# Seven-product output projection: weight sums made earlier and kept in DRAM, y combinations made beside the attention output, evictions in steps

## The chip, the cores and the metric

One core of one Trainium2 chip runs the whole program. The time is device microseconds (us) of one execution; runs are compared by their median. The engines are named as in the profile: PE is TensorE (matmuls; PEld are its weight loads), DVE is VectorE, ACT is ScalarE, POOL is GpSimd, and SP is SyncE, whose queue issues all the transfers of this kernel.

## The reference

A decoder layer on 512 tokens of width 2048: an attention branch and a gated delta branch run beside each other, are merged by two sigmoid gates, and go through an output projection. What matters here is the end of each:

```python
    y_a = a_out @ w_o_swa
    ...
    y_b = o.reshape(B, T, DN_VAL).astype(x.dtype) @ w_o_dn

    y = jax.nn.sigmoid(mg_a) * y_a + jax.nn.sigmoid(mg_b) * y_b
    return x + gate * (y @ w_out)
```

`w_out` is 2048 x 2048, `w_o_dn` 4096 x 2048, `w_o_swa` 2048 x 2048, all float32.

## The kernel before, in words

**Precision.** Every large product is made of three fp32r matmuls (`mm3`, lines 221 to 226): each operand is split into a high and a low part (`split`, lines 50 to 53: a cast on ACT, a subtraction on DVE), and high x high, high x low and low x high are added in PSUM.

**Weights.** `plan` (line 141) writes out one list of jobs, each a weight tile of 128 x 2048. `load_job` (179) loads a job into one of two buffers `raw`; `split_half` (188) splits half of it (1024 columns) into one of three pairs `whi`, `wlo`; `half` hands a half out by name. Loads and splits are set off by `half_done` and `weight_tick`, so that they run ahead of the matmuls: a load is issued when the second half of the job two before it has been split.

**Order of work.** The program is laid out by hand as a sequence of tiles (`channel_tile`, 228: 16 blocks kt of three matmuls, 48 in all). After every second kt it calls `pump` (81), which gives other work, written as generators, its next step: `go` by a count of ticks, `paced` by a budget per tick against the cost that the generator yields, `beside` by a rate. This sets the order in which the instructions are written down; the compiler's scheduler then puts each engine's queue in an order of its own, and may bring an instruction forward when its buffer and its data are free.

**Stages.** Start, delta branch, then three stages at the end that the change touches:

- *Delta output* (`branch_b`, 924). Twice (`half`): 16 blocks of the delta branch's output are loaded as `oraw` (line 938, two buffers) and split into `oh` and `ol`; two merge gate tiles `ma`; then 16 tiles `od`, whose matmuls need all 16 blocks. The first half's results go to `yb_d` in DRAM, the second half adds to them. Beside it `gate` (1418) loads 16 tiles `gw` of 1 MB, one buffer, and adds each to `gate_bc` on DVE.
- *Attention output* (`finish`, 1213). 16 tiles `os`. Each tile j is merged with its gates into y (128 channels x 512 tokens, `m`) and stored to `y_d`. y is cut in four quadrants (channels below and above block 8, tokens `lo` and `hi`), and of the seven left factors of the product scheme five are made and split here: a11, s3, a12, s1, s2.
- *Output projection* (`output`, 1277). y @ w_out by a scheme with seven products m1 to m7 of half-size matrices instead of eight, for each of two column blocks n. An item is one quarter of a product (p, 2 kt, 12 matmuls); 2 x 7 x 4 items. The right factors are quadrants of `w_out` and four sums of them: the sums are made on DVE in place just ahead of their split (`add`, line 1297; `prep`, 1317), in the buffers a, b and c, loaded by `load` (1290). The last two left factors a22 and s4 are made meanwhile by `combos` (1254) from `y_d`: loads of `ya` and `yc`, sums and low parts on POOL (1272, 1274, 1263), casts on ACT (1262). `evict` (1358) combines a finished product with the ones kept; `columns` (1349) multiplies by the gate (DVE, 1352), loads x (1354), adds it on POOL (1355) and stores (1356). A product's whole eviction is written down at one point, in the middle of the first item after it.

Of the kernel before, what the change touches and what calls it, by code (L numbers as in the profile page):

```python
# [7 lines left out]
F32 = mybir.dt.float32  # L8
# [8 lines left out]
P = 128  # L17
# [15 lines left out]
NFIRST = 4  # L33
STW = 320 + NST * P


class Layer:
# [103 lines left out]
    def plan(self):  # L141
# [28 lines left out]
        jobs += [(f"out{i}", a["w_out"][0, i]) for i in range(2)]  # L170
# [90 lines left out]
    def build(self):  # L261
        tc, nc, a = self.tc, self.nc, self.a
        with ExitStack() as es:
# [4 lines left out]
            self.v_d = self.dram.tile([2, P, T], F32, name="v_d")  # L268
            self.wraw = es.enter_context(tc.tile_pool(name="wraw", bufs=2, reuse_waits="tile"))
# [654 lines left out]
    def branch_b(self):  # L924
        tc, nc, a = self.tc, self.nc, self.a
        with ExitStack() as es:
# [5 lines left out]
            self.beside(self.gate(wk, pg), 0.2, "gate")  # L932
            oh = op.tile([P, KT, T], F32R, name="oh")
# [20 lines left out]
            self.drain("gate")  # L954
        self.dump("yb", self.yb_d)


# [255 lines left out]
    def finish(self):  # L1213
        tc, nc, a = self.tc, self.nc, self.a
        with ExitStack() as es:
# [4 lines left out]
            yp.tile([P, 504], F32, name="aligny")  # L1220
            lo, hi = slice(0, 256), slice(256, 512)
            with ExitStack() as eo:
                self.pmm = eo.enter_context(tc.tile_pool(name="pmmf", bufs=2, space=PSUM, reuse_waits="tile"))
                for j in range(KT):
# [10 lines left out]
                    nc.sync.dma_start(out=self.y_d[j], in_=m)  # L1235
                    put = lambda n, src: self.split(A[n][0][:, j % 8, :], A[n][1][:, j % 8, :], src)
                    put("a11" if j < 8 else "a12", m[:, lo])
                    if j < 8:
                        nc.vector.tensor_tensor(out=yb[:, lo], in0=m[:, lo], in1=m[:, hi], op=ALU.add)
                        put("s3", yb[:, lo])  # L1240
                    else:
# [8 lines left out]
            for n in ("a22", "s4"):  # L1250
                A[n] = quad(fx, n)
            self.output(es, wk, fx, A)

    def combos(self, wk, A):

        nc = self.nc
        lo, hi = slice(0, 256), slice(256, 512)
        TT = nc.gpsimd.tensor_tensor

        def put(n, kt, src):  # L1260
            h, l = A[n][0][:, kt, :], A[n][1][:, kt, :]
            nc.scalar.copy(out=h, in_=src)
            TT(out=l, in0=src, in1=h.bitcast(F32), op=ALU.subtract)

        for kt in range(8):
            p = wk.tile([P, T], F32, tag="m", name="ya")
            nc.sync.dma_start(out=p, in_=self.y_d[kt])
            q = wk.tile([P, T], F32, tag="yb", name="yc")
            nc.sync.dma_start(out=q, in_=self.y_d[kt + 8])
            yield  # L1270
            put("a22", kt, q[:, hi])
            TT(out=p, in0=p, in1=q, op=ALU.subtract)
            yield
            TT(out=p[:, lo], in0=p[:, lo], in1=p[:, hi], op=ALU.add)
            put("s4", kt, p[:, lo])

    def output(self, es, wk, fr, A):
# [3 lines left out]
        slots = {}  # L1281

        def load(slot, c, r, nchunk, parts=(0, 1)):

            for i in parts:
                if slot == "a":
                    t = self.wraw.tile([P, 2048], F32, tag="raw", name="raw")
                else:
                    t = fr.tile([P, 2048], F32, tag=f"{slot}{i}", name=f"raw{slot}")
                nc.sync.dma_start(out=t, in_=a["w_out"][2 * c + nchunk, 2 * r + i])  # L1290
                slots[slot, i] = t

        piece = lambda slot, p: slots[slot, p // 2][:, (p % 2) * 1024 : (p % 2) * 1024 + 1024]

        def add(x, y):
            def f(p):
                nc.vector.tensor_tensor(out=piece(x, p), in0=piece(x, p), in1=piece(y, p), op=ALU.add)

            return f

# [222 lines left out]
```

## Time and profile before

| | |
|---|---|
| median of 3 runs | 2995.43 us (2982.93 to 2997.62) |
| profiled execution | 2993.07 us, its span 2991.3 us |
| PE busy | 2881.6 us, 96% |
| DVE busy | 1790.8 us, 60% |
| ACT busy | 1084.1 us, 36% |
| POOL busy | 281.9 us, 9% |
| moved by DMA | 450.07 MB, mean 150 GB/s |

Times are microseconds from the first instruction. "Busy" is the sum of an engine's instructions; matmuls are pipelined, so that a new one starts every 0.23 us though each lasts 0.39. A groups row has the line, engine and operation, the tiles out<-in, shapes and count, then busy us and mean ns of one, then the idle time of the engine just before them and what ended it. A waits row reads "who line <- what it waited for: us in total, times, longest". The stages lie at about 1683 to 2082 us (delta output), 2640 to 2807 (attention output) and 2807 to the end (output projection).

### The profile page before, as it was taken

The page shows a single profiled execution, that of the slowest core. Times are in us where ns is not written, and L with a number is a line of the kernel's source. Part 1 is how long each engine was busy: PE and PEld are TensorE (multiplying, and loading weights), DVE is VectorE, ACT ScalarE, POOL GpSimd, SP SyncE. Part 2 cuts the span into 40 slices and gives each one's busy share as a digit, 9 for nine tenths or more (in the row PEclk, how much of TensorE's full clock was granted, in tenths as well). Part 3 has the DMA queues.
Part 4 walks back from the last instruction along what each step waited for, and adds up shares of the span by engine and source line. Part 5 has one row for each costly group of instructions (what it writes and reads, how often), then busy time and mean ns, then how long its engine had stood idle before and what let it go on. Part 6 is the DMA issues. An engine that isn't in the chain of part 4 may idle for free.

```text
span 2991.3 us, 37937 instructions
## 1 busy us (share of the span) xinstructions
PE 2881.6 (96%) x14524; PEld 2358.0 (79%) x14524; DVE 1790.8 (60%) x2863; ACT 1084.1 (36%) x2101; POOL 281.9 (9%) x236
## 2 busy tenths in 40 slices
PE   6899989999999999999999999999999999999988
PEld 5587777778788888888888788888788788888767
DVE  5765898898544444455544453433755655554787
ACT  3355333333433333333333322312234434432333
POOL 0012220210000000001000000000100000000251
PEclk8999999999999999999999999999999999999999
DMA  9855635633533333343332575555322223355652
GB/s 335 308 173 176 182 130 168 187 102 121 154 125 107 121 107 124 113 136 113 123 124 85 190 265 197 200 167 164 104 87 87 74 101 101 112 202 183 217 169 85
DMA packets 175079, 450.07 MB, mean 150 GB/s; under 512 B 74129, under 2 KB 76689, under 8 KB 139057
## 3 DMA queue, kind: packets, MB, share of 16 engines
q1 hardware_dynamic: 174898, 447.66, 45.4%
q8 instruction: 114, 1.87, 0.3%
q14 instruction: 67, 0.55, 0.1%
HBM read 385.90 MB, written 59.46 MB: 149 GB/s over the span
## 4 chain that ended last, share of the span: by engine, by line
PE 77%; DVE 10%; DMA 6%; POOL 2%; issue 2%; ACT 2%; SPq 1%; POOLq 0%; DVEq 0%; ACTq 0%
PE mm L224 21%; PE mm L226 21%; PE mm L225 21%; DVE wlo L53 2%; DVE atmp L708 2%; DVE A L714 1%; DMA E<-g_rows 1%; DVE wa L390 1%; PE S L1150 1%; ACT whi L52 1%; PE O L1201 1%; PE pv L861 1%; PE po L880 1%; PE pP L258 1%; DMA oraw<-o_d 1%
## 5 line engine op out<-in xcount | busy, mean ns | idle before, releaser
L224 PE MATMUL mm<-hh,whi 128*128 128x512 f32 x2784 | 1136.6, 408 | 0.7 <-ACT mth L247 0.7
L226 PE MATMUL mm<-hh,wlo 128*128 128x512 f32 x2784 | 1094.2, 393 | 0.0
L225 PE MATMUL mm<-hl,whi 128*128 128x512 f32 x2784 | 1093.1, 393 | 0.0
L53 DVE TENSOR_TENSOR wlo<-raw,whi 128x1024 fp32r<-128x1024 f32 (+1 forms) x452 | 555.4, 1231 | 501.3 <-ACT whi L52 486.4
L52 ACT CAST whi<-raw 128x1024 fp32r<-128x1024 f32 (+1 forms) x452 | 470.6, 1043 | 947.8 <-PE mm L225 894.6
L226 PEld LDWEIGHTS mm<-hh,wlo 128*128 128x128 f32 x2784 | 525.5, 189 | 113.7 <-issue 0.4
L224 PEld LDWEIGHTS mm<-hh,whi 128*128 128x128 f32 x2784 | 527.0, 189 | 110.6 <-issue 8.4
L225 PEld LDWEIGHTS mm<-hl,whi 128*128 128x128 f32 x2784 | 527.8, 190 | 99.7 <-issue 0.8
L224 PE MATMUL mm<-oh,whi 128*128 128x512 f32 x512 | 200.6, 393 | 2.0 <-ACT oh L52 1.0
L225 PE MATMUL mm<-ol,whi 128*128 128x512 f32 x512 | 199.6, 390 | 1.0 <-DVE ol L53 1.0
L226 PE MATMUL mm<-oh,wlo 128*128 128x512 f32 x512 | 199.5, 390 | 0.5 <-DVE wlo L53 0.5
L808 POOL TENSOR_TENSOR qe<-qe,yq 128x512 f32<-128x512 f32 x32 | 50.1, 1586 | 929.0 <-DMA qe<-eg_rows 868.7
L677 POOL TENSOR_TENSOR E<-E,neg_g 128x512 f32<-128x512 f32 x64 | 76.1, 1189 | 488.0 <-DMA E<-g_rows 416.1
L224 PEld LDWEIGHTS mm<-oh,whi 128*128 128x128 f32 x512 | 96.2, 188 | 24.0 <-ACT oh L52 2.0
L225 PEld LDWEIGHTS mm<-ol,whi 128*128 128x128 f32 x512 | 96.2, 188 | 22.6 <-DVE ol L53 2.0
L226 PEld LDWEIGHTS mm<-oh,wlo 128*128 128x128 f32 x512 | 96.2, 188 | 21.0 <-DVE wlo L53 1.2
L708 DVE TENSOR_TENSOR atmp<-A 128x62 f32<-128x62 f32 (+30 forms) x124 | 111.0, 895 | 2.0
L714 DVE TENSOR_TENSOR A<-A,atmp 128x62 f32<-128x62 f32 (+30 forms) x124 | 109.5, 883 | 1.8
L854 DVE SCALAR_TENSOR_TENSOR r<-pp,neg_eg,vt 128x128 f32<-128x128 f32 x96 | 29.2, 346 | 81.2 <-PE pp L851 79.4
L553 DVE SCALAR_TENSOR_TENSOR yv<-mm,convh,yv 128x511 f32<-128x511 f32 (+2 forms) x96 | 71.4, 744 | 8.1 <-ACT yv L550 6.7
L1174 ACT ACTIVATE sm<-sm,mx,rs 128x256 f32<-128x256 f32 (+1 forms) x128 | 71.7, 562 | 3.3 <-DVE mx L1169 3.3
L390 DVE SCALAR_TENSOR_TENSOR wa<-wa,silu_cb 128x2048 f32<-128x2048 f32 x24 | 54.8, 2282 | 7.1 <-DMA silu_cb<-silu_d 7.1
(350 smaller groups left out, 3179.4 us busy)
## 6 DMA issues: line engine op xcount, KB each, us to landing
raw<-in_w_ch SPq DMA_DIRECT2D x158, 1024.0 KB
wa<-in_w_ada_ss SPq DMA_DIRECT2D x32, 1024.0 KB
raw<-in_w_od SPq DMA_DIRECT2D x32, 1024.0 KB
E<-g_rows SPq DMA_DIRECT2D x64, 256.0 KB
gw<-in_w_ada_gate SPq DMA_DIRECT2D x16, 1024.0 KB
raw<-in_w_os SPq DMA_DIRECT2D x16, 1024.0 KB
qe<-eg_rows SPq DMA_DIRECT2D x32, 256.0 KB
o_d<-zh SPq DMA_DIRECT2D x32, 256.0 KB
```

Of the source, the lines that this page charges most:

```text
L52: self.nc.scalar.copy(out=hi, in_=src)
L53: self.nc.vector.tensor_tensor(out=lo, in0=src, in1=hi.bitcast(F32), op=ALU.subtract)
L224: nc.tensor.matmul(ps, lhsT=wh, rhs=xh, start=first, stop=False)
L225: nc.tensor.matmul(ps, lhsT=wh, rhs=xl, start=False, stop=False)
L226: nc.tensor.matmul(ps, lhsT=wl, rhs=xh, start=False, stop=last)
L390: nc.vector.scalar_tensor_tensor(out=wa, in0=wa, scalar=1.0, in1=scb, op0=ALU.mult, op1=ALU.mult, accum_out=t[:, j : j + 1])
L553: nc.vector.scalar_tensor_tensor(out=y[:, s:], in0=ps[:, : T - s], scalar=w[:, j : j + 1], in1=y[:, s:], op0=ALU.mult, op1=ALU.add)
L677: nc.gpsimd.tensor_tensor(out=E, in0=E, in1=ng, op=ALU.add)
L708: eng.tensor_tensor(out=t, in0=A[:, m : m + 1, m + 1 :].to_broadcast([P, m, n]), in1=A[:, :m, m : m + 1].to_broadcast([P, m, n]), op=ALU.mult,
L714: eng.tensor_tensor(out=A[:, :m, m + 1 :], in0=A[:, :m, m + 1 :], in1=t, op=ALU.add)
L808: nc.gpsimd.tensor_tensor(out=qf, in0=qf, in1=q, op=ALU.mult)
L1174: nc.scalar.activation(t, t, AF.Exp, scale=r[:, h : h + 1], bias=mx[:, h : h + 1], accum_out=den[:, h : h + 1])
```

## The change

1. *Weight sums.* A new generator `weight_sums` runs beside the delta output stage (`paced`, budget 1 per tick). In eight turns it loads four half tiles (128 x 1024) of the quadrants of `w_out`, makes the four sums on DVE in place, and stores them to a DRAM tile `f_d`. Its buffers q00, q10, q11, q01 are single. In `output` all 28 right factors are ordinary jobs of the weight list: quadrants from `w_out`, sums from `f_d`. Jobs of this stage use five buffers in turn, the two `raw` and three new ones `rawo`.
2. *y combinations.* a22 and s4 are made and split for each j from 8 on in the attention output stage (ACT and DVE) and stored, four parts of 128 x 256, to a DRAM tile `c_d`; y is stored to `y_d` for j below 8 only. In `output` they are loaded into `late`, during m5 and m2 of n = 0. `combos` is gone, and POOL has no work in the stage.
3. *Evictions.* `evict` is a generator. One step of it is taken after each half of an item, and the row block t is now the outer loop within an item, kt the inner one. x is loaded during the product that needs it (four buffers), and added on DVE. The gate rows are loaded during m7.

```diff
+PRODUCTS = [
+    ("m1", "a11", (0, 0), None),
+    ("m7", "s3", None, 1),
+    ("m5", "s1", None, 0),
+    ("m2", "a12", (0, 1), None),
+    ("m6", "s2", None, 2),
+    ("m4", "a22", None, 3),
+    ("m3", "s4", (1, 1), None),
+]
...
-        jobs += [(f"out{i}", a["w_out"][0, i]) for i in range(2)]
+        self.out0 = len(jobs)
+        for n in range(2):
+            for m, (_, _, q, f) in enumerate(PRODUCTS):
+                for i in range(2):
+                    src = a["w_out"][2 * q[0] + n, 2 * q[1] + i] if q else self.f_d[n, f, i]
+                    jobs.append((f"out{n}_{m}_{i}", src))
...
-            raw = self.wraw.tile([P, 2048], F32, tag="raw", name="raw")
+            own = j < self.out0 or (j - self.out0) % 5 < 2
+            pool, tag = (self.wraw, "raw") if own else (self.oraw, "rawo")
+            raw = pool.tile([P, 2048], F32, tag=tag, name="raw")
...
+            sums = self.paced(self.weight_sums(wk), 1.0)
...
             self.drain("gate")
+            self.drain_slow(sums)
...
+    def weight_sums(self, wk):
+        nc = self.nc
+        for n in range(2):
+            for i in range(2):
+                for h in range(2):
+                    cols = slice(h * 1024, (h + 1) * 1024)
+                    q = []
+                    for c, r in ((0, 0), (1, 0), (1, 1), (0, 1)):
+                        t = wk.tile([P, 1024], F32, tag=f"q{c}{r}", name=f"q{c}{r}", bufs=1)
+                        nc.sync.dma_start(out=t, in_=self.a["w_out"][2 * c + n, 2 * r + i][:, cols])
+                        q.append(t)
+                    yield 10.0
+                    for f, (x, y) in enumerate(((0, 1), (1, 2), (0, 2), (2, 3))):
+                        nc.vector.tensor_tensor(out=q[f], in0=q[x], in1=q[y], op=ALU.add)
+                        nc.sync.dma_start(out=self.f_d[n, f, i][:, cols], in_=q[f])
+                        yield 6.0
...
                         put("s2", q[:, lo])
+                        late = wk.tile([P, 4, 256], F32R, tag="late", name="late", bufs=1)
+                        self.split(late[:, 0, :], late[:, 1, :], m[:, hi])
+                        s4 = wk.tile([P, 256], F32, tag="s4", name="s4", bufs=1)
+                        nc.vector.scalar_tensor_tensor(
+                            out=s4, in0=q[:, lo], scalar=-1.0, in1=m[:, lo], op0=ALU.mult, op1=ALU.subtract
+                        )
+                        self.split(late[:, 2, :], late[:, 3, :], s4)
+                        nc.sync.dma_start(out=self.c_d[j - 8], in_=late.bitcast(F32))
...
+        late = fx.tile([P, 8, 4, 256], F32, name="late")
+        for k, s in enumerate(("a22", "s4")):
+            A[s] = tuple(late[:, :, 2 * k + x, :].bitcast(F32R) for x in range(2))
+        self.oraw = es.enter_context(tc.tile_pool(name="oraw", bufs=3, reuse_waits="tile"))
+        for _ in range(3):
+            self.load_job()
...
+        def finish_columns(n, c, t, src, sign):
...
+            STT(out=src, in0=src, scalar=sign, in1=gts[n][:, c, :], op0=ALU.mult, op1=ALU.mult)
+            TT(out=src, in0=src, in1=xs.pop((n, c, t)), op=ALU.add)
             nc.sync.dma_start(out=self.out[t * P : (t + 1) * P, csl], in_=src)
...
+            if p == 1 and rows(n, name):
+                load_x(n, name)
...
+            if n == 0 and m in (2, 3):
+                kt = 4 * (m - 2) + p
+                nc.sync.dma_start(out=late[:, kt], in_=self.c_d[kt])
+            hi, lo = self.half(f"out{n}_{m}_{p // 2}")
             ah, al = A[s]
+            for t in range(2):
+                tsl = slice(t * P, (t + 1) * P)
+                for kk in range(2):
+                    kt = 2 * p + kk
+                    w = slice(kk * T, kk * T + T)
                     self.mm3(ps[name, t], (ah[:, kt, tsl], al[:, kt, tsl]), (hi[:, w], lo[:, w]), kt == 0, kt == 7)
+                if t == 0:
+                    self.half_used += 1
+                    while self.half_split < min(self.half_used + 2, 2 * len(self.jobs)):
+                        self.split_half()
+                    self.weight_tick()
+                if steps and next(steps[0], True):
+                    steps.pop(0)
             if p == 3:
+                steps.append(evict(n, name))
```

More of the change, by code (lines that the diff above doesn't have):

```diff
@@ L1356, in columns, with rows, load_x @@
             nc.sync.dma_start(out=self.out[t * P : (t + 1) * P, csl], in_=src)
+        def rows(n, name):
+            return {"m2": (0, 0), "m6": (1, 2), "m4": (0, 2), "m3": (1, 0)}.get(name)
+        def load_x(n, name):
+            c, t0 = rows(n, name)
+            csl = slice(c * 1024 + n * T, c * 1024 + n * T + T)
+            for t in range(t0, t0 + 2):
+                x = fx.tile([P, T], F32, tag="x", name="x", bufs=4)
+                nc.sync.dma_start(out=x, in_=a["x"][t * P : (t + 1) * P, csl])
+                xs[n, c, t] = x
@@ L1384, in evict @@
                     TT(out=k, in0=b, in1=k, op=ALU.subtract)
[L1385 removed]
+                    finish_columns(n, 0, 2 + t, k, 1.0)
                 elif name == "m3":
@@ L1388, in evict @@
                     TT(out=k, in0=b, in1=k, op=ALU.add)
-                    columns(n, 1, t, k, -1.0)
-        for i in range(2):
-            prep(i)
+                    finish_columns(n, 1, t, k, -1.0)
+                yield
         for i, (n, m, p) in enumerate(items):
-            name, s, slot, _ = order[m]
+            name, s = PRODUCTS[m][:2]
             if p == 0:
```

132 lines of the change are left out of this document (22 added, 110 removed).

## The prediction

> **What bounds the kernel now.** The page gives the span. In these fences the columns of a windows row are the stretch in us, its length, then busy us (and instructions) of PE, PEld, DVE, ACT and POOL, the granted clock, the busy share of the DMA engines and GB/s.
>
> ```profile
> span 2991.3 us, 37937 instructions
> ```
>
> The page's busy times make TensorE the bound, so a stage is worth looking at only where TensorE waits. The busy times by stretch show where that is:
>
> ```profile
> 1683.00:1702.00 19.00, 19.00 (x86) 15.73 (x85) 8.57 (x10) 7.54 (x11) 0.00 (x0) 1.00 0.84 300
> 1702.00:1736.00 34.00, 30.52 (x128) 22.93 (x127) 20.16 (x18) 10.31 (x15) 0.00 (x0) 1.00 0.79 271
> 2640.00:2806.90 166.90, 166.90 (x738) 138.19 (x737) 79.00 (x120) 46.65 (x68) 2.81 (x2) 1.00 0.55 178
> 2806.90:2821.20 14.30, 12.65 (x55) 9.88 (x54) 13.42 (x15) 6.64 (x11) 2.44 (x2) 1.00 0.95 362
> 2806.90:2983.90 177.00, 161.40 (x673) 128.85 (x671) 151.61 (x134) 66.52 (x81) 68.74 (x44) 0.96 0.46 156
> ```
>
> The first two rows are the head of the delta output stage, the third is the attention output stage (no wait at all), the last the seven-product output projection, where DVE is busy 151.61 of 177 us and the clock falls to 0.96. Its matmuls, from the timeline (start, duration):
>
> ```profile
> 2806.86 0.39 PE L224 MATMUL m<-whi,a11h 128*128 128x512 f32 x1
> ...
> 2817.51 0.39 PE L226 MATMUL m<-whi,a11l 128*128 128x512 f32 x1
> ...
> 2983.52 0.39 PE L226 MATMUL m<-whi,s4l 128*128 128x512 f32 x1
> ```
>
> The first two lines are the first and last of the 48 matmuls of m1: 10.65 / 47 = 0.2266 us each. The program has 14 products x 8 kt x 2 row blocks x 3 = 672, so the last should start 671 x 0.2266 = 152.1 us after the first. It starts 176.7 us after: **24.6 us are lost**. The waits of this stage (total us, times, longest) say to whom:
>
> ```profile
> ACT s4h L1262 <- POOL ya L1274: 20.3, 6, 6.3
> ...
> PE m L224 <- ACT whi L52: 8.4, 4, 3.6
> PE m L225 <- DVE wlo L53: 7.2, 6, 1.5
> ```
>
> TensorE's two rows make 15.6 us of idle time. The other 9.0 us are matmuls at the lower clock behind such gaps. Two things make the weight halves late: the sums of w_out quadrants on DVE (L1297), and the casts of the y combinations on ACT (L1262), which wait for POOL with the weight casts queued behind them. The chain of waits has the second case:
>
> ```profile
> 2859.14 0.69 POOL ya L1274
> 2859.89 0.27 issue
> 2860.16 1.05 ACT whi L52
> 2861.23 2.15 DVE wlo L53
> ```
>
> **The change, part by part.**
>
> *Sums and combinations leave the output stage.* The sums are four groups of eight passes, the costliest shown first, so up to 48 us of DVE. The next row is what a DVE pass over 128x1024 takes over the whole program, the last one over 128x256.
>
> ```profile
> L1297 DVE TENSOR_TENSOR rawb<-rawb,raw 128x1024 f32<-128x1024 f32 x8 | 12.1, 1518 | 0.3
> ```
>
> ```profile
> L53 DVE TENSOR_TENSOR wlo<-raw,whi 128x1024 fp32r<-128x1024 f32 (+1 forms) x452 | 555.4, 1231 | 501.3 <-ACT whi L52 486.4
> ```
>
> ```profile
> L53 DVE TENSOR_TENSOR s3l<-yb,s3h x8: 424/426/426, 2647.6 to 2723.7; 128x256 fp32r<-128x256 f32 x8
> ```
>
> Both makers of late halves go, and with them every idle us of the stage: **-24.6 us**. What DVE then has to do is 56 splits of 1.23 (69 us) and 60 eviction passes of about 0.69 (41 us): 110 of 152 us. The x additions that come to it from POOL are among them, 16 x 0.69 = 11 us. Paced, an item of 2.72 us gets at most one split and two steps of three passes, 1.23 + 4.14 = 5.4 us. That is 2.7 us late, against a ring of three halves that is one item, 2.72 us, ahead. I put this at nothing, with 2 us if the cover is gone.
>
> *The tail.* After the last matmul come two DVE passes for each row block, the POOL addition and the store:
>
> ```profile
> 2983.27 1.37 DVE L1388 TENSOR_TENSOR m<-m,m 128x512 f32<-128x512 f32 x2 [3.97 <-PE m L226]
> 2984.55 1.28 DVE L1352 SCALAR_TENSOR_TENSOR m<-m,gt 128x512 f32<-128x512 f32 x2
> 2985.31 2.86 POOL L1355 TENSOR_TENSOR m<-m,x 128x512 f32<-128x512 f32 x2 [4.87 <-DVE m L1352]
> 2986.98 1.56 SPq L1356 DMA_DIRECT2D out<-m  x2
> ```
>
> POOL ends at 2988.17, 4.3 us after the last matmul (2983.9). With the row block as the outer loop, the first block's bank is done 6 x 0.2266 = 1.4 us earlier. Six DVE passes of 0.65 from 1.4 us before the end finish 2.6 us behind it: **-1.5 us**. Removed in all: 26 us.
>
> *Attention output stage.* Blocks 8 to 15 get two more splits and a sum over 128x256 (3 x 0.43 = 1.3 us of DVE, 0.8 of ACT) and a 512 KB store in place of a 256 KB one, per 10.9 us. DVE is busy 79.0 of 166.9 us there: nothing, as TensorE keeps two halves in hand.
>
> *Sums in the delta output stage.* DVE gets 32 x 1.23 = 39 us over 36 tiles of 10.9 us, some 390 us, and has half of its time free (8.57 busy of 19 us and 20.16 of 34 at the head): nothing by itself. The transfers are another matter. Each of eight turns loads 4 x 512 KB and stores 4 x 512 KB, 4.19 MB, all on SP's queue. Transfers there are served in the order of issue, as the start of the output stage shows:
>
> ```profile
> 2806.83 0.33 SPq L1290 DMA_DIRECT2D rawb<-in_w_out  x1
> ...
> 2811.15 0.45 SPq L1269 DMA_DIRECT2D yc<-y_d  x1
> ```
>
> ```profile
> 2811.15 10.08 DMA yc<-y_d
> ...
> 2980.90 3.25 DMA x<-in_x
> ```
>
> ```profile
> rawb<-in_w_out SPq DMA_DIRECT2D x8, 1024.0 KB
> ...
> yc<-y_d SPq DMA_DIRECT2D x8, 256.0 KB
> ```
>
> A 256 KB load lands 10.08 us after issue when four of 1 MB and two of 256 KB stand before it (4.98 MB with itself, from 2806.83 to 2821.2: 347 GB/s), and 3.25 us after issue when nothing does. The most the engines moved is the 362 GB/s of the row of 2806.90 above, at a share of 0.95.
>
> Nor does the pace of the loop hold a load back. The loop asks for 34 ticks, of six matmuls or 1.36 us each, for one turn: 46 us. But the queue issues a load once its buffer is free:
>
> ```profile
> 1683.20 0.95 SPq L938 DMA_DIRECT2D oraw<-o_d  x2
> 1684.19 0.43 SPq L1424 DMA_DIRECT2D gw<-in_w_ada_gate  x1
> ...
> 1747.99 0.43 SPq L938 DMA_DIRECT2D oraw<-o_d  x1
> ```
>
> ```profile
> 1735.48 0.69 DVE L53 TENSOR_TENSOR ol<-oraw,oh 128x512 fp32r<-128x512 f32 x1
> ```
>
> The load at 1747.99 belongs to the second half, 130 us later in the program. So the first four quadrant loads will go out at about 1684, behind the first two oraw and ahead of the rest. There they meet the one place of the stage without slack. The 16 oraw loads go two at a time, eight round trips, to the last split at 1735.48, and TensorE has by then used up what it can do without the last block. It has two merge tiles (to 1702) and, with three weight halves in hand, three output tiles less their last 3 kt, 45 x 0.68 = 30.6 us; the trace has 30.52 busy of 34. Any delay of that chain is TensorE's delay.
>
> Its size: the first two rows of the busy times hold 19 x 300 + 34 x 271 = 14.9 MB in 53 us. A turn of the sums takes own transfers of 11.6 us at 362 GB/s, 7.2 us for one gate, one weight and two oraw loads queued between, about 5 us of sums, and two landings of 2.5 us (3.25 less 0.7 of transfer): some 28 us, 0.15 MB per us. The chain's time t follows from 14.9 + 0.15 t = 0.362 t: 70 us, **+17 us**. Ends: nothing, if the loads come late or slowly; 8 x 5.8 = 47 us, if a whole 2.1 MB stands before every round trip. I take the 17, as both rates are rows. **+2 us** go with it for the lower clock behind the gaps (9.0 us fell to ten waits before).
>
> Behind SP's new waits (a store for its DVE sum) stand the weight loads (L184), issued two tiles, 22 us, ahead. DVE's sums wait for their loads with the splits behind them, one half (5.4 us) ahead. I count nothing for these; 0 to 10 us belongs in the range.
>
> *New loads of the output stage.* It takes 28 loads of 1 MB instead of 16, eight of 512 KB (late), and the x and gate rows sooner. Nearly all may issue at 2806.9, when h is freed. Three raws, late and its last store, x, the gate rows and the next three raws are 12.5 MB, 34.5 us at 362 GB/s: with a landing of 2 us the last of these, the eighth weight load, is there at 2843. Each load feeds 24 matmuls, 5.44 us, and its first half must be begun 2.3 us ahead (cast 1.05, split 1.23): 2806.9 + 7 x 5.44 - 2.3 = 2842.7. Slack is near zero: **+3 us**, between 0 and 8.
>
> **Sum.** -24.6 - 1.5 + 17 + 2 + 3 = -4 us on the profiled execution, which takes 2993.07 us (span 2991.3 and 1.8 around it). The median of the runs is 2995.43, 2.4 above it; I carry the difference over: 2991 us. About 0.5%, 15 us, is what a measurement of this kernel can tell from no change.
>
> **The rivals.**
>
> *B, the gain is kept.* The sums come at the loop's pace, 4.19 MB in 46 us: 14.9 + 0.091 t = 0.362 t gives 55 us, a delay of 2. Then -26 + 2 + 3 = -21: 2974 us, 2969 if the output stage costs nothing. For it: the DMA share of 0.79 leaves room. Against it: the early load at 1747.99.
>
> *C, slower.* The oraw chain is stretched by a whole burst in each of the eight round trips, +47 us: -26 + 47 + 2 + 3 = +26, 3021 us. It shows as slower once the chain loses more than 15 + 26 - 5 = 36 us, six of the eight trips. For it: strict order of service, and oraw always issued last, after a split. Against it: a turn takes longer than two round trips, so not every trip meets a burst.
>
> *D, the sums' traffic costs less than its bytes.* Half of it is stores. If the engines take these beside the loads, the chain has 14.9 + 0.075 t = 0.362 t, 52 us, and no delay: -26 + 3 = -23, 2972 us. For it speaks only that the row of 0.95 is nearly all loads; against it, that the rows with stores among them (0.84 for 300, 0.79 for 271) move no more per share than that one. A page of the Trainium skill points the same way: "DMA: Bandwidth & Descriptors", section "Bandwidth", has 425 GB/s for one core that loads 16 MB. By it the first equation, 14.9 + 0.15 t = 0.425 t, gives 54 us and a delay of 1. The trace doesn't agree so far: 362 at a share of 0.95.
>
> *E, the pace does nothing at all.* This is the forecast's own mechanism; if DVE's wait for the quadrants also holds the splits, its 10 us give 3001, still within the bound.
>
> **How the numbers follow.** Forecast with E (gain eaten by the chain, 2980 to 3010, within 0.5%): 0.45. B: 0.32, as the place and size of the bursts are inferred and a delay under 9 us already shows as faster. D: 0.06. C: 0.17. The range from 2966 (B and nothing lost) to 3014 takes in the forecast, B and D, and the lower part of C. Faster 0.32 + 0.06 = 0.38, same 0.45, slower 0.17.
>
> **What would show it.** In the profile after: matmuls of the output projection without waits, 152 us from first to last (right if under 157); no POOL there; the last store issued within 3.5 us of the last matmul. At 1684, four quadrant loads before the third oraw; the last oraw split near 1752 instead of 1736, with TensorE waiting for the cast of oh on ACT and the DMA share above 0.9. If that split stays near 1736, my chain is wrong and B has it; if it comes after 1772, C. Waits of DVE for quadrant loads with splits behind them would be the cost that I left at nothing.

## The result, and the profile after

| | before | after |
|---|---|---|
| median of the runs | 2991.01 us (2982.93 to 2997.62, 8 runs) | 2969.20 us (2965.54 to 2977.24, 8 runs) |
| profiled execution | 2993.07 us, span 2991.3 | 2965.54 us, span 2963.8 |

The ratio of the times is 0.9931 [0.9914, 0.9948]: about 21 us less, just beyond the 0.5% that the prediction set as what a measurement of this kernel can tell. It lies in the predicted range, but it is rival B's result (the gain is kept), not that of the forecast. The profiled execution is the fastest of its eight runs, so its span shows 27.5 us less where the medians show 21.8.

The windows of the kernel after, stretch by stretch, with the columns explained above (stretch, length, busy us of PE, PEld, DVE, ACT and POOL, granted clock, DMA share, GB/s):

```profile
1681.00:1700.00 19.00, 19.00 (x85) 15.75 (x84) 11.92 (x13) 7.18 (x10) 0.00 (x0) 1.00 0.82 273
1700.00:1735.00 35.00, 32.29 (x127) 24.07 (x127) 17.95 (x18) 13.08 (x19) 0.00 (x0) 0.95 0.90 325
1740.00:1820.00 80.00, 80.00 (x355) 66.24 (x354) 43.74 (x30) 19.29 (x22) 0.00 (x0) 1.00 0.92 331
2637.00:2804.50 167.50, 167.50 (x741) 138.69 (x740) 85.55 (x141) 52.15 (x82) 0.00 (x0) 1.00 0.57 188
2804.50:2820.00 15.50, 15.50 (x70) 12.85 (x69) 10.11 (x16) 9.02 (x13) 0.00 (x0) 1.00 0.98 399
2804.50:2962.00 157.50, 153.09 (x676) 126.43 (x674) 105.33 (x124) 62.90 (x67) 0.00 (x0) 1.00 0.72 261
```

The first two rows are the head of the delta output stage. It carries 19 x 273 + 35 x 325, 16.6 MB, where it carried 14.9 MB, in about the same time. The attention output stage (fourth row) took the new splits without a wait. The fifth row is the start of the output projection: 399 GB/s at a share of 0.98, and TensorE busy throughout. The last row is the output projection with its tail: no POOL, and a clock of 1.00 where it was 0.96.

The same stage in the timeline (start, duration): its first and last matmul, and what follows the last.

```profile
2805.11 0.39 PE L240 MATMUL m<-whi,a11h 128*128 128x512 f32 x1
...
2957.20 0.39 PE L242 MATMUL m<-whi,late 128*128 128x512 f32 x1
2957.63 0.69 DVE L1360 TENSOR_TENSOR m<-m,m 128x512 f32<-128x512 f32 x1
2958.24 0.68 DVE L1317 TENSOR_TENSOR m<-m,x 128x512 f32<-128x512 f32 x1
2958.83 0.69 DVE L1316 SCALAR_TENSOR_TENSOR m<-m,gt 128x512 f32<-128x512 f32 x1
2958.94 1.66 SPq L1318 DMA_DIRECT2D out<-m  x2
2959.55 0.69 DVE L1317 TENSOR_TENSOR m<-m,x 128x512 f32<-128x512 f32 x1
```

From first to last matmul it is 152.09 us, which is 671 x 0.2267: nothing is lost any more, against 176.7 before. From the end of the last matmul (2957.6) to the end of the span it is 6.2 us, against 7.4 (2983.9 to 2991.3).

The loss that was expected at the head of the delta output stage did not come. SP's queue there, from the timeline:

```profile
1681.32 0.95 SPq L956 DMA_DIRECT2D oraw<-o_d  x2
1682.32 0.90 SPq L987 DMA_DIRECT2D q<-in_w_out  x2
1686.42 0.93 SPq L956 DMA_DIRECT2D oraw<-o_d  x2
1687.40 0.90 SPq L987 DMA_DIRECT2D q<-in_w_out  x2
1693.00 0.93 SPq L956 DMA_DIRECT2D oraw<-o_d  x2
1693.98 0.42 SPq L1408 DMA_DIRECT2D gw<-in_w_ada_gate  x1
...
1723.04 0.97 SPq L956 DMA_DIRECT2D oraw<-o_d  x2
1724.06 0.43 SPq L200 DMA_DIRECT2D raw<-in_w_od  x1
1724.53 0.43 SPq L992 DMA_DIRECT2D f_d<-q  x1
1725.00 0.65 SPq L987 DMA_DIRECT2D q<-in_w_out  x1
...
1735.52 1.59 SPq L987 DMA_DIRECT2D q<-in_w_out  x3
```

The four loads of the first turn did go out at once, as predicted, two behind each pair of oraw. But the second turn starts only at 1725 to 1735, some 43 us later, and behind a store and a weight load. Over all eight turns it is 42 us on average (31 to 60). That is near the pace of the loop, 46 us, and not the 28 us of the forecast. The gate loads gave way. Their first and last start, from the views of the tile gw, before and after:

```profile
L1424 SPq DMA_DIRECT2D gw<-in_w_ada_gate x16: 327/330/430, 1684.2 to 1815.8; - x16
```

```profile
L1408 SPq DMA_DIRECT2D gw<-in_w_ada_gate x16: 327/408/753, 1694.0 to 1883.7; - x16
```

The same 16 MB were spread over 190 us instead of 132, a load every 12.6 us instead of every 8.8; the rate of their generator, one load per ten ticks of 1.36 us, is 13.6. The gate is needed only in the output projection, and TensorE did not wait for it. The last oraw split comes in the pair that starts at 1730.43 on DVE, against 1735.48 before:

```profile
1730.43 1.29 DVE L62 TENSOR_TENSOR ol<-oraw,oh 128x512 fp32r<-128x512 f32 x2
```

The whole stage, in the windows from 1675 to 2090 us, before and after:

```profile
1675.00:2090.00 415.00, 411.34 (x1807) 336.80 (x1806) 176.39 (x178) 107.96 (x132) 1.00 (x2) 1.00 0.60 205
```

```profile
1675.00:2090.00 415.00, 411.73 (x1796) 336.16 (x1795) 213.30 (x208) 107.50 (x128) 1.00 (x2) 1.00 0.82 284
```

TensorE's busy time is the same. The share of the DMA engines rose from 0.60 to 0.82 and DVE took 37 us more, both into time that stood free.

So 24.6 + 1.2 us of the 27.5 come from the output projection and its tail. The other 1.7 us are there ahead of the output projection, which starts at 2805.11 instead of 2806.86; already the first oraw load starts at 1681.3 instead of 1683.2, before the change has done anything.

### The profile page after: what moved, and what is told of

Its sections match the earlier page's. It is cut to its first block, busy times and chain, and to the rows that moved or that the text cites. A ratio compares the mean times of both kernels' runs of the same rounds, so it can differ in the third digit from the quotient of the medians.

```text
span 2963.8 us, 38016 instructions
## 1 busy us (share of the span) xinstructions
PE 2875.7 (97%) x14524; PEld 2356.0 (79%) x14524; DVE 1787.3 (60%) x2903; ACT 1086.4 (37%) x2101; POOL 206.8 (7%) x188
## 5 line engine op out<-in xcount | busy, mean ns | idle before, releaser
L62 DVE TENSOR_TENSOR wlo<-raw,whi 128x1024 fp32r<-128x1024 f32 (+1 forms) x484 | 589.3, 1219 | 511.9 <-ACT whi L61 492.1
L61 ACT CAST whi<-raw 128x1024 fp32r<-128x1024 f32 (+1 forms) x484 | 504.6, 1044 | 974.9 <-PE mm L241 864.4
L240 PEld LDWEIGHTS mm<-oh,whi 128*128 128x128 f32 x512 | 96.2, 188 | 25.8 <-ACT whi L61 2.7
```

Source lines behind the costliest of these rows:

```text
L61: self.nc.scalar.copy(out=hi, in_=src)
L62: self.nc.vector.tensor_tensor(out=lo, in0=src, in1=hi.bitcast(F32), op=ALU.subtract)
L240: nc.tensor.matmul(ps, lhsT=wh, rhs=xh, start=first, stop=False)
```

## The experiments

Each was run beside the kernel before, on the same chip as it, though not on one chip for all. So the ratios count: they are to the kernel before, and "to the change" is the difference of a ratio to 0.9931, times 2991 us. A ratio is known to about 0.0015, which is 4.5 us. By their times alone, e4, e5, e6 and e7 can't be told from the change; what is said of e4 and e5 below rests on their traces.

| | median, us | ratio to before [95%] | to the change, us |
|---|---|---|---|
| e1_sums_unused | 2997.54 | 1.0019 [1.0010, 1.0028] | (before + 6) |
| e5_combos_only | 2975.18 | 0.9943 [0.9928, 0.9958] | +4 |
| e4_combos_back | 2973.89 | 0.9940 [0.9925, 0.9955] | +3 |
| e11_combos_dve | 2982.57 | 0.9971 [0.9959, 0.9983] | +12 |
| e6_evict_whole | 2971.00 | 0.9928 [0.9913, 0.9943] | -1 |
| e2_no_pace | 3063.66 | 1.0233 [1.0215, 1.0252] | +90 |
| e9_no_pace_pool | 3016.68 | 1.0081 [1.0064, 1.0098] | +45 |
| e3_double | 3024.62 | 1.0112 [1.0096, 1.0128] | +54 |
| e8_oraw1 | 3023.20 | 1.0103 [1.0088, 1.0118] | +51 |
| e12_gate_first | 2999.37 | 1.0031 [1.0020, 1.0041] | +30 |
| e7_oraw3 | 2967.50 | 0.9918 [0.9903, 0.9932] | -4 |
| e13_oraw3_later | 2962.42 | 0.9898 [0.9881, 0.9914] | -10 |

The theory after the result was B: the sums come at the loop's pace into free time of the engines, and the gain is kept whole. Its rival was the forecast's mechanism in a smaller form: the head loses something to the sums, and the gain elsewhere is larger than 26 us.

### What the sums cost: e1_sums_unused

The kernel before, with the new generator beside its delta output stage. The output projection is that of before and does not read the sums.

```diff
+            sums = self.paced(self.weight_sums(wk), 1.0)
...
+            self.drain_slow(sums)
```

> The kernel before, with the weight sums of the change made beside the delta output stage and stored, but read by nobody. It measures what the sums cost that stage by themselves. The chain theory of the prediction (every turn's 4.19 MB lies ahead of the oraw loads): 17 to 19 us slower than before, 3010 us, last oraw split of the first half near 1752. The pace theory, formed on the trace after (the generator's pace keeps it to one turn per 40 to 50 us, and the gate loads give way): no difference, within 5 us of before, last oraw split near 1735 and the first half's TensorE waits near 4 us.

It was slower by 0.0019 [0.0010, 0.0028], which is 3 to 8 us and not 17. Its profiled execution is the fastest of its ten runs, with a span of 2989.4 us. It has no more TensorE gaps in the stage than the kernel before (5.7 us between 1675 and 2090, against 6.0, counting gaps over 0.3 us), so it doesn't show where the few us of the median go. Other traces show a part: from the first oraw load to the first matmul of the output projection it is 1122.7 to 1126.6 us in the four with the sums at this pace (e1, the change, e4, e6; all with two oraw buffers), and 1121.4 to 1123.7 in the three without (before, e5, e11). That is some 3 us in the mean, as far as seven traces can tell. The sums themselves ran as alone, from the view of their tile:

```profile
L975 DVE TENSOR_TENSOR q<-q,q x32: 1217/1224/1227, 1692.1 to 1992.5; 128x1024 f32<-128x1024 f32 x32
```

### What made the 24.6 us: e5_combos_only, e4_combos_back, e11_combos_dve, e6_evict_whole

*e5*: before, with the y combinations alone moved to the attention output stage and loaded from `c_d`; the weight sums stay on DVE in the output projection.

```diff
+                        late = wk.tile([P, 4, 256], F32R, tag="late", name="late", bufs=1)
+                        self.split(late[:, 0, :], late[:, 1, :], m[:, hi])
...
-        side = self.combos(wk, A)
...
-                    next(side, None)
```

> The kernel before with part 2 alone: a22 and s4 made in the attention output stage and loaded into late; weight sums on DVE just ahead of their splits, evictions and the x addition on POOL as before. If the sums are nearly the whole cause (combos back cost only 4.7 us): at most 5 us faster than before, 2986 us. If either part alone removes most of the loss, since POOL's combos and DVE's sums only hurt when they meet: 15 to 20 us faster, 2971 to 2976 us, with the sums' mean near 1.25 us in place of 1.35 to 1.52. If the two causes simply add up as the prediction had it: 13 us faster, 2978 us.

*e4*: the change, with the y combinations back in the output projection on POOL and ACT; the weight sums stay where the change put them.

```diff
-                        self.split(late[:, 0, :], late[:, 1, :], m[:, hi])
...
+        side = self.combos(wk, A)
...
+                    next(side, None)
```

> The changed kernel with a22 and s4 made in the output projection again, by combos on POOL and ACT from y_d, in place of the loads of late; sums and evictions as changed. The two-causes theory (combos' casts hold up the weight casts on ACT, sums hold up DVE, each by itself): the excess before a12 comes back, 12 to 13 us of the 24.6, so 2981 us. Rival (POOL was only slow because it met DVE's sums; without them combos are harmless): within 4 us of after.

With the sums alone in the stage (e5) the 672 matmuls start over 158.0 us, 5.9 more than the 152.1 without waits:

```profile
2808.92 0.39 PE L224 MATMUL m<-whi,a11h 128*128 128x512 f32 x1
...
2966.95 0.39 PE L226 MATMUL m<-whi,late 128*128 128x512 f32 x1
```

With the combinations alone (e4) it is 155.2, 3.1 more. With both, before, it was 24.6 more. The two do not add: by these figures 15.6 us came from their being there together. But e4 also keeps the change's evictions, its five load buffers and the x additions on DVE. So the 3.1 is what the combinations cost there; what they would cost beside the old evictions without the sums was not run. In the groups the same sum, a pass over 128x1024, is shorter without POOL's combinations beside it (two of four groups in e5; before, in the order of these rows, 1490 and 1518 ns):

```profile
L1308 DVE TENSOR_TENSOR raw<-raw,rawb 128x1024 f32<-128x1024 f32 x8 | 10.7, 1354 | 0.0
L1308 DVE TENSOR_TENSOR rawb<-rawb,raw 128x1024 f32<-128x1024 f32 x8 | 9.8, 1224 | 0.3
```

and POOL's pass is shorter without DVE's sums (before, then e4):

```profile
L1272 POOL TENSOR_TENSOR ya<-ya,yc 128x512 f32<-128x512 f32 x8 | 15.9, 1989 | 329.5 <-ACT whi L52 316.5 <-DMA yc<-y_d 13.0
```

```profile
L1309 POOL TENSOR_TENSOR ya<-ya,yc 128x512 f32<-128x512 f32 x8 | 12.2, 1519 | 329.4 <-ACT whi L61 316.4 <-DMA yc<-y_d 12.9
```

These are means of two kinds of pass. One by one, in the kernel before, the 22 sums that began while POOL stood still took 1.21 to 1.23 us. The other 10 began during a POOL pass and took 1.63 to 2.31, and each ended 1.08 us after that pass did (one 1.09). POOL's long pass stretches in the same way, to 2.26 us beside DVE's from 1.26 alone. From the timeline of before (start, duration; put in order of time):

```profile
2821.39 2.25 POOL L1272 TENSOR_TENSOR ya<-ya,yc 128x512 f32<-128x512 f32 x1 [10.64 <-DMA yc<-y_d]
2822.42 2.31 DVE L1297 TENSOR_TENSOR raw<-raw,rawb 128x1024 f32<-128x1024 f32 x1
2823.61 1.72 POOL L1263 TENSOR_TENSOR a22l<-yc,a22h 128x256 fp32r<-128x256 f32 x1
2824.65 1.75 DVE L1297 TENSOR_TENSOR rawb<-rawb,rawc 128x1024 f32<-128x1024 f32 x1
```

So these passes did their work one after the other, though their records overlap.

ACT's wait for POOL, which the prediction had as the second maker of late halves, is still there in e4, but its longest is 3.9 us and not 6.3, and TensorE waits for no weight cast of ACT and only 2.0 us for DVE's splits:

```profile
ACT s4h L1299 <- POOL ya L1311: 17.5, 7, 3.9
```

Either POOL's passes beside DVE's cost the time, or DVE with the sums simply has too much to do. *e11* tells these apart: before, with the passes of the combinations on DVE instead of POOL, so that DVE has more to do and POOL less.

```diff
-        TT = nc.gpsimd.tensor_tensor
+        TT = nc.vector.tensor_tensor
```

> The kernel before with the sums and low parts of combos on DVE in place of POOL; nothing else is changed, and no work is left out. It gives DVE 8 x (0.69 + 3 x 0.43) = 16 us more in the output projection and leaves POOL only the x additions. Meeting theory (the 24.6 us come from POOL's and DVE's passes slowing each other, 1.35 to 1.52 us for a sum that takes 1.22 alone and 1.98 us for a combination that takes 1.52 without the sums): faster than before by 5 to 15 us, 2980 us. Load theory (DVE has too much to do beside the weight splits, and any more makes it worse): slower than before by 5 us or more.

It is 9 us faster than before, though DVE does all of it. Its matmuls start over 164.0 us, 11.9 more than without waits:

```profile
2806.04 0.39 PE L224 MATMUL m<-whi,a11h 128*128 128x512 f32 x1
...
2970.07 0.39 PE L226 MATMUL m<-whi,s4l 128*128 128x512 f32 x1
```

So with the sums on DVE in all three kernels, the loss is 5.9 us with the combinations away, 11.9 with them on DVE, and 24.6 with them on POOL. The windows of the stage, e5 and then e11, say what POOL spared DVE:

```profile
2808.90:2967.40 158.50, 154.29 (x673) 125.49 (x671) 139.77 (x138) 62.32 (x67) 26.68 (x14) 1.00 0.51 177
2806.00:2970.50 164.50, 155.81 (x673) 125.12 (x672) 151.16 (x164) 67.15 (x81) 26.03 (x14) 1.00 0.51 168
```

DVE was busy 139.8 us without the combinations, 151.2 with them, and 151.6 before, when POOL had them (last row of the prediction's busy times). POOL did the work and DVE was busy as long. This rules out that DVE merely had too much to do. The way by which POOL cost more shows in TensorE's waits: for DVE's splits they are 7.2 us before and 8.2 in e11, for ACT's weight casts 8.4 and 0.4. So what e11 gains comes by way of the casts, which before stood behind a cast that waited for POOL, up to 6.3 us. That POOL was late because it took turns with DVE is argued from the passes: the long one took 2.08 to 2.26 us six times of eight before, and 1.28 to 1.54 six times of eight in e4, without the sums. The row that is left in e11:

```profile
PE m L225 <- DVE wlo L53: 8.2, 7, 1.7
```

*e6*: the change, with each product's eviction written whole at its first step.

```diff
-                if steps and next(steps[0], True):
-                    steps.pop(0)
+                    for f in steps:
+                        for _ in f:
+                            pass
+                    steps.clear()
```

> The changed kernel with each product's eviction written down at one point again, in the middle of the first item after it, in place of one step per half item. The prediction counted the evictions' steps at nothing with 2 us if the cover is gone: 0 to 4 us slower than after. Rival (the steps are what makes the sums' removal pay, since a whole m6 eviction is 12 passes, 8 us of DVE, against a ring that is one item of 2.7 us ahead): 2 column blocks x about 5 us of waits at m6 and more at the others, with the low clock behind them 10 to 15 us slower, 2981 us.

No difference (0.9928 and 0.9931, the intervals almost the same), and its waits of the output projection have no row of TensorE either. Pacing the evictions brings nothing that can be measured once the sums are gone from DVE.

### What holds the sums' traffic off the critical path: e2, e9, e3, e8, e12

*e2_no_pace*: the change, with no cost asked for a turn.

```diff
-                    yield 10.0
+                    yield 0.0
...
-                        yield 6.0
+                        yield 0.0
```

> The changed kernel with the two costs that the generator of the sums yields set to 0, so that all eight turns are written down at the first tick. Pace theory: the turns follow each other as fast as their single buffers come free, some 28 us or less each, the oraw chain of the first half is stretched by 17 us or more, and the kernel is 15 to 40 us slower than after (2985 to 3010 us). Rival (the engines have room, or the order of the queue protects oraw whatever the pace): within 5 us of after, 2969 us.

The loss is larger than was expected, and it is not where the forecast had put it. The turns now came 11 to 21 us apart, and still the oraw chain wasn't stretched: its last split started at 1726.2, 43 us after the first load, against 50 in the change. The gate loads gave way here too (the first went out at 1801.8), and it didn't help. The weight loads were late. All 64 transfers of the sums stood in SP's queue ahead of the next `raw`, which was issued at 1802.3. The waits from 1680 to 1900 us:

```profile
ACT whi L61 <- DMA raw<-in_w_od: 86.9, 2, 81.6
PEld mm L240 <- ACT whi L61: 84.0, 1, 84.0
PE mm L240 <- ACT whi L61: 83.3, 1, 83.3
```

*e9_no_pace_pool*: the same, with the loads and stores of the sums on GpSimd's queue, so that nothing of SP's stands behind them.

```diff
-                        nc.sync.dma_start(out=t, in_=self.a["w_out"][2 * c + n, 2 * r + i][:, cols])
+                        nc.gpsimd.dma_start(out=t, in_=self.a["w_out"][2 * c + n, 2 * r + i][:, cols])
...
-                        nc.sync.dma_start(out=self.f_d[n, f, i][:, cols], in_=q[f])
+                        nc.gpsimd.dma_start(out=self.f_d[n, f, i][:, cols], in_=q[f])
```

> The kernel without a pace (costs 0, which was 94 us slower than after), with the quadrant loads and the stores of the sums issued by GpSimd's queue in place of SP's. Queue theory (SP takes its queue in the order written, and the weight loads stood behind 64 transfers of the sums that wait for single buffers): the weight loads go out in time, and most of the loss is gone: 2970 to 2995 us. Bandwidth theory (the engines are full with the sums' bytes wherever they are issued): 3030 us or more. Between them, both count.

Half of e2's loss goes, half stays. The queue's order was one half. The other is put down to crowding, as the engines were busy to 0.93 from 1680 to 1740 (0.86 in the change); that is argued, not shown by a run of its own. It falls on both streams, weights and oraw (last split 1747.2, some 63 us after the first load, against 50 in the change). The waits from 1675 to 2100 us:

```profile
ACT whi L61 <- DMA raw<-in_w_od: 55.5, 7, 13.7
...
ACT oh L61 <- DMA oraw<-o_d: 41.0, 16, 8.0
```

*e3_double*: every turn made twice at half the cost, 33.6 MB more in the same time; the first copy goes to a DRAM tile that nobody reads.

```diff
-        for n in range(2):
-            for i in range(2):
+        for n, i, dst in [(n, i, d) for n in range(2) for i in range(2) for d in (self.f2_d, self.f_d)]:
+            if True:
...
-                    yield 10.0
+                    yield 5.0
...
-                        nc.sync.dma_start(out=self.f_d[n, f, i][:, cols], in_=q[f])
-                        yield 6.0
+                        nc.sync.dma_start(out=dst[n, f, i][:, cols], in_=q[f])
+                        yield 3.0
```

> The changed kernel with every turn of the sums made twice (the second time into a DRAM tile that nobody reads) at half of the yielded costs, so 16 turns in the same time and 33.6 MB more. Bandwidth theory: the stage moves 115 MB in 399 us after the change; 149 MB need 414 us at 360 GB/s and 450 us at 331 GB/s, so 15 to 50 us slower than after, 2985 to 3020 us. Rival (the weight loads keep their place in the queue and only the gate loads and the sums give way, which run on to the end of the stage): within 10 us of after, 2979 us or less.

The first 33.6 MB cost a few us at most (e1), the second 54. At the 331 GB/s of the row of 1740 the second are 101 us of transfer, so about half found room. The queue has a part in it again: from 1735 to 1860 SP's queue stood 72 us for the sums and their buffers, 4 in the change, at the same DMA share of 0.91. How the 54 us divide between queue and bytes is open. Late again are the weights (1675 to 2100 us):

```profile
ACT whi L61 <- DMA raw<-in_w_od: 147.1, 21, 15.7
```

*e8_oraw1*: the change, with one buffer for oraw instead of two, to see whether that chain has the slack that the forecast denied.

```diff
-                    raw = wk.tile([P, T], F32, tag="oraw", name="oraw")
+                    raw = wk.tile([P, T], F32, tag="oraw", name="oraw", bufs=1)
```

> The changed kernel with one buffer for oraw in place of two, so that the 16 loads of each half go one by one. Chain theory of the prediction (TensorE has used up all other work when the last block is split, so any delay of this chain is TensorE's): 16 trips of about 5.3 us take 85 us instead of 46, about 35 us slower in the first half and less in the second, 3000 us or more. Rival (there is slack that I didn't see): within 8 us of after, 2977 us.

The last oraw split moved from 1731 to 1774.3, 43 us, and the time by 51: a delay of this chain is TensorE's delay, as was said. The waits (1675 to 2100 us) now name it:

```profile
ACT oh L61 <- DMA oraw<-o_d: 97.7, 26, 7.9
...
PE mm L240 <- ACT oh L61: 33.9, 16, 5.6
```

*e12_gate_first*: the change, with the gate loads asked for at five times the rate, so that they cannot give way.

```diff
-            self.beside(self.gate(wk, pg), 0.2, "gate")
+            self.beside(self.gate(wk, pg), 1.0, "gate")
```

> The changed kernel with the gate's generator at a rate of 1.0 in place of 0.2, so that its 16 loads of 1 MB stand five times earlier in the program and don't fall behind the sums. It tests whether the sums cost nothing because the gate loads gave way. If so: the head of the stage has the sums on top of the gate loads, as the prediction had it, and 17 us or more are lost: 2985 to 3000 us. Rival (the queue's order would give oraw and the weights their turn all the same): within 5 us of after, 2969 to 2974 us.

30 us are lost. The gate loads now end at 1849.2 instead of 1883.7. oraw is on time all the same (last split 1727.8); it is the weights that are late, and the gate's own matmul, which this edit brings forward too, waits on DVE. From 1680 to 1900 us:

```profile
ACT whi L61 <- DMA raw<-in_w_od: 76.0, 13, 11.8
...
PE pgate L1422 <- DVE gate_bc L1414: 7.2, 1, 7.2
```

In the change the first of these rows is 6.4 us in 4 waits. The engines were not full: from 1735 to 1860 they moved 289 GB/s at a share of 0.84, against 327 at 0.91 in the change. SP's queue stood still, for 85 of these 125 us, ahead of gate loads that waited for their one buffer, with the weight loads written down behind them (the queue's own waits, 1735 to 1860):

```profile
SPq L1408 <- DMA gw<-in_w_ada_gate: 56.6, 11, 6.7
SPq L1408 <- DVE gate_bc L1414: 28.9, 12, 2.4
```

In the change these two rows are 24.9 us together. So it is the place of the gate loads in the queue, ahead of weight loads, that costs here; that they make room by their bytes is not what this run shows. The kernel before was not run with the faster gate, so the part of the 30 us that the sums have in it is open.

### A better head: e7_oraw3, e13_oraw3_later

*e7*: the change with three oraw buffers. *e13*: besides, the sums begin 40 ticks later, when the oraw chain is through, and are a little denser.

```diff
-                    raw = wk.tile([P, T], F32, tag="oraw", name="oraw")
+                    raw = wk.tile([P, T], F32, tag="oraw", name="oraw", bufs=3)
```

```diff
+        yield 40.0
...
-                    yield 10.0
+                    yield 9.0
...
-                        yield 6.0
+                        yield 5.0
```

> The changed kernel with three buffers for oraw in place of two. One buffer cost 54 us, so the chain of these loads sets TensorE's pace at the head of the stage; the trace after shows some 4 us of TensorE waits there (two of them for a weight cast, not for oh). Chain theory: with a load more in flight the waits for oh go, 2 to 4 us faster than after, 2966 us. Rival (what is left at the head waits for weight loads, which a deeper oraw chain can only delay): no gain, 2969 us or some us slower.

> The changed kernel with three oraw buffers, and the sums begun 40 ticks (54 us) later at 29 ticks a turn in place of 34, so that the head of the stage holds no sums. If the head's last 4 us of waits are due to transfers that crowd each other: 3 to 5 us faster than after, 2965 us. If the denser turns behind it crowd the weight loads, or the waits have another cause: 2969 us or slower.

e7 can't be told from the change. e13 is the fastest of all, 0.9898 [0.9881, 0.9914]; the interval only just touches that of the change, and it overlaps that of e7. In both runs the last oraw split starts at 1720, 32 and 36 us after the first load, against 50 in the change. So the third buffer shortens the chain with the sums beside it or without; what their later start adds is not shown. The windows of e13 show the head without a wait, where the change had 32.29 busy of 35 us at a clock of 0.95 and the kernel before 30.52 of 34:

```profile
1700.00:1735.00 35.00, 35.00 (x154) 28.33 (x153) 22.67 (x21) 12.71 (x18) 0.00 (x0) 1.00 0.89 332
1735.00:1800.00 65.00, 65.00 (x289) 53.83 (x288) 33.27 (x24) 15.54 (x18) 0.00 (x0) 1.00 0.91 317
```

## Why the prediction was right and wrong

*Sums and combinations leave the output stage, -24.6 us:* right to the tenth, since the count of matmuls by their spacing gave the time without waits. The explanation of the 24.6 by two separate makers was wrong: the sums alone make 5.9 us (e5), the combinations 3.1 beside the change's evictions (e4), and most of the rest comes with POOL's passes taking turns with DVE's, which goes with late casts on ACT (e11). A page of the Trainium skill, "SBUF — State Buffer", section "Who interferes with whom", says that a DVE instruction with two SBUF inputs contends with a GpSimd instruction that reads SBUF; the traces agree, with 1.21 to 1.23 us for a sum alone and 1.63 to 2.31 for one that began during a POOL pass. The prediction's 1518 ns is a mean of both kinds.

*The tail, -1.5 us:* -1.2 measured.

*Attention output stage and evictions, nothing:* right for both (no wait in 167.5 us; e6).

*The oraw chain, +17 us, and its low clock, +2:* this is the step that failed. Its first half, that the chain has no slack, holds (e8). Its second half was "Nor does the pace of the loop hold a load back", with a turn of 28 us and all other traffic unchanged. The turns came 42 us apart on average, and the chain took 50 us from the first load to the last split, against 52 before and 70 in the forecast. The mistake was to read the early load at 1747.99 as a queue without order. In e2 a weight load went out only after all 64 transfers written down ahead of it, so a load goes out in its place in SP's queue. That the load at 1747.99 had an early place is the reading that fits this; the second turn of the sums had its place behind a store and a weight load. The other half of the mistake was to keep the gate loads at their rate of before. They ended 68 us later (1883.7 instead of 1815.8) without a wait of TensorE. Even without a pace, in e2, the chain was not stretched, while the weight and gate loads stood still. Only in e9, where the sums have a queue of their own and all streams run beside each other, is it 13 us longer than in the change, near the forecast's 17.

*Who is late when the engines or the queue are full:* the forecast named oraw. In e2, e3 and e12 it is the weight loads; the first half's oraw chain suffers beside them only in e9. The rival C, slower by a burst in each round trip, was right that unpaced traffic costs tens of us and wrong about the victim. The 0 to 10 us left open for the weight loads behind SP's new waits is where the danger lay. For rival D, that stores cost less than their bytes, nothing speaks: the rows with the sums' stores move 331 GB/s at a share of 0.92, the row of 2804.5 without them 399 at 0.98.

*New loads of the output stage, +3 us:* nothing. The slack was worked out with 362 GB/s as the most the engines move; the row of 2804.5 has 399 at a share of 0.98. The landing of 2 us used there is from no row; the prediction's other landings are 2.5.

*The sum:* -24.6 - 1.2 + 0 + 0 = -25.8 against -27.5 measured on the profiled executions, the other 1.7 us being there ahead of the stage. By the medians it is -21.8, about 4 us less than -25.8, and e1 says that the sums cost 3 to 8 us. So rival B has the mechanism, and the time lies in the range because the range took in B, not because of the forecast. That B's remark "if the output stage costs nothing" has the median to the us is luck: its 2969 is 26 us below the 2995.43 of the first three runs, and the eight runs of the result put the kernel before at 2991.01. Where the few us of e1 go is shown only in part. The lower end of the range, 2966, is called "B and nothing lost", which by the prediction's sum is 2969.

## What to carry to other kernels

Added traffic need not add to the time. First find the transfers with slack: here the gate loads moved by 68 us and TensorE did not wait. Then find the streams that stand behind the new transfers in the same queue: here the weight loads, which became late in e2, e3 and e12. Before saying that a pace does nothing, see what stands ahead of the paced load in its queue. When two causes of a wait are taken away together, try each alone: here most of the wait came from both being there at once.

## What the runs showed of the hardware

- The DMA engines moved 399 GB/s at a share of 0.98 in the first 15.5 us of the output projection, mostly loads of 1 MB, but 322 to 338 at 0.90 to 0.94 where the sums' loads and stores of 512 KB were among them (the change from 1740 to 1880, e2 from 1735 to 1790). Whether the stores or the smaller pieces make the difference was not tried. The page "DMA: Bandwidth & Descriptors" of the Trainium skill, section "Bandwidth", has 425 for one core; the prediction said that the trace did not agree, and this row comes closer to it.
- 64 transfers of 512 KB, waiting in one queue for their buffers and sums, held the weight loads behind them, so that ACT waited 81.6 us for one; TensorE did nothing at all from 1735 to 1790 us. On a queue of their own they cost half as much (45 us against 90). In e12 single-buffered gate loads did the same: SP's queue stood 85 of 125 us, at a DMA share of 0.84.
- A DVE sum over 128x1024 took 1.21 to 1.23 us alone; one that began during a POOL pass took 1.63 to 2.31 and ended 1.08 us after that pass. With the sums on DVE, the output projection lost 5.9 us with the combinations away, 11.9 with them on DVE as well and 24.6 with them on POOL, and DVE was busy 151.2 us with them on it, 151.6 with them on POOL.
